# Scaling token tiles by 1/rms inside their transposing product, with a diagonal matrix in place of the identity

## The chip, the cores and the metric

The kernel runs on one core of one Trainium2 chip. The metric is device microseconds of one execution, the median over several runs. Engines are called as the profile calls them: PE is TensorE (PEld its weight loads), DVE is VectorE, ACT is ScalarE, POOL is GpSimd, SP is SyncE, which issues the transfers here.

## The reference

One layer of a hybrid backbone in float32: 1024 latent tokens `x` and 256 context tokens `ctx`, 1024 features each. Both are normed and modulated, multiplied by one input matrix, and feed a windowed attention and a bidirectional mLSTM; an output projection and a SwiGLU block follow. The change touches only the first step:

```python
def rms_norm(x, g):
    xf = x.astype(jnp.float32)
    y = xf * lax.rsqrt(jnp.mean(xf * xf, axis=-1, keepdims=True) + EPS)
    return (y * g.astype(jnp.float32)).astype(x.dtype)

def modulate(h, shift, scale):
    return h * (1.0 + scale) + shift

px = modulate(rms_norm(x, g_pre_mix[layer]), sh_m, sc_m) @ w_in[layer]
pc = modulate(rms_norm(ctx, g_pre_mix[layer]), csh_m, csc_m) @ w_in[layer]
```

A token has one factor 1/rms over all its features; gain, scale and shift are one number per feature.

## The kernel before, in words

Tokens are worked on in ten tiles of 128: tiles 0 to 7 are `x`, 8 and 9 are `ctx`. The projections need them transposed, features on partitions, and split into a high and a low part (`hh`, `hl`; `ch`, `cl` for the context) whose type, fp32r, takes one pass on TensorE; three products of such parts (lines 70 to 72) stand for one of full precision.

The first stage (line 224) multiplies the conditioning vectors by two sections of `w_ada`, streamed in eight tiles each; of the result come `scol` and `hcol`, one column of scale and of shift for each of 8 feature tiles (lines 235 to 249). With these each token tile i is prepared:

- `prep_a(i)`: load `xt` (line 183, one of four buffers, so tile i + 4 waits for tile i's last reader); ScalarE squares it and sums each row into `st` (line 185), writing its junk where `hraw` will be; square root and reciprocal give 1/rms, one number per partition (lines 176, 177); GpSimd multiplies `xt` by it in place (line 187).
- `prep_b(i)`: eight transposes of 128 x 128 against the identity `ident` (line 200), four to a tile `pt` in PSUM; VectorE multiplies each `pt` by `scol` into `hraw` (line 202); GpSimd, for tile 0 VectorE, adds `hcol` (line 203); `split` casts the high part on ScalarE (line 58) and subtracts for the low part on VectorE (line 59).
- `s1(i)`: 24 slab products of 272 columns (lines 70 to 72) give gates and some values (lines 277 to 282).

Then `gates()` works out the mLSTM gates in small steps, while TensorE runs a second slab of 384 columns for the ten tiles; `ml_weights` (lines 386 to 390) loads rows of the result, exponentiates and stores them, tile by tile. After that 13 projections of 128 columns follow in `tproj` (lines 441 to 444). The first two are convolved in `conv`: ScalarE copies the result out of PSUM to `cr` (lines 455, 458), VectorE makes three operations of it, first on 1024 latent columns, then on 256 context columns (lines 460 to 462). Beside them `ada_rest` takes the other sections of `w_ada` without TensorE: eight loads `wb` into two buffers and a product-and-add on VectorE for each (lines 491, 492; `wb_0` to `wb_7`).

The order on each engine is not the order of the code. A scheduler with its own model of the time writes it when the program is built; each engine then runs its list strictly in that order. So a change of one operation moves others.

Of the kernel before, what the change touches and what calls it, by code (L numbers as in the profile page):

```python
# [9 lines left out]
F32 = mybir.dt.float32  # L10
# [4 lines left out]
ADD, SUB, MUL, MAX, MIN = ALU.add, ALU.subtract, ALU.mult, ALU.max, ALU.min  # L15

P = 128
# [20 lines left out]
def body(tc, x, ctx, vecs, bcv, bada, gqm, gqf, wada, ws1, ws2, wt, wout, wfi, wfo,  # L38
         const, cosc, sinc, out):
    nc = tc.nc  # L40
    pe, act, dve, pool = nc.tensor, nc.scalar, nc.vector, nc.gpsimd
# [14 lines left out]
    def split(hi, lo, raw):  # L56

        act.copy(hi, raw)  # L58
        dve.tensor_tensor(lo, raw, hi.bitcast(F32), SUB)  # L59
# [18 lines left out]
    def hcast(t, n=4, w=P):  # L78

        return t.rearrange("p (h o) -> p h o", o=1).broadcast_to([t.shape[0], n, w])  # L80
# [13 lines left out]
    st = c.tile([P, 64], F32, name="st")  # L94
# [9 lines left out]
    ident = cst[:, CID:CID + P]  # L104
# [14 lines left out]
    def R(k, name, shape, dt=F32):  # L119
        t = rp[1].tile([P, 1152 if k < 4 else 1024], dt, name=name, tag=f"r{k}")  # L120
        n = int(np.prod(shape))
        v = t[:, 0:n]
        if len(shape) == 2:
            v = v.rearrange("p (a b) -> p a b", b=shape[1])
        elif len(shape) == 3:
            v = v.rearrange("p (a b c) -> p a b c", b=shape[1], c=shape[2])
        elif len(shape) == 4:
            v = v.rearrange("p (a b c d) -> p a b c d", b=shape[1], c=shape[2], d=shape[3])
        return v
# [28 lines left out]
    q1 = p1[1]  # L158
    w1h = [q1.tile([P, 4, 384], F32R, name=f"w1h{i}")[:, :, 0:272] for i in range(2)]
    w1l = [q1.tile([P, 4, 384], F32R, name=f"w1l{i}")[:, :, 0:272] for i in range(2)]  # L160

    q1.tile([P, 64], F32, name="padw")
    cs4 = q1.tile([P, KT, 4], F32R, name="cs4")
    cz4 = q1.tile([P, KT, 4], F32, name="cz4")
# [4 lines left out]
    def w2_tile(part, i, name):  # L169
        return q1.tile([P, 4 * 384], F32R, name=name, tag=f"w2{part}{i}")  # L170

    xts, hraw, xd = {}, {}, {}

    def rms_r(dst, ss):

        act.activation(dst, ss, AF.Sqrt, bias=epst, scale=1.0 / D)
        dve.reciprocal(dst, dst)

    def prep_a(i):

        j = i - NT
        xt = xts[i] = R(4 + i % 4, f"xt{i}", (D,))
        xd[i] = dma(xt, x[i * P:(i + 1) * P] if i < NT else ctx[j * P:(j + 1) * P])
        hraw[i] = R((12, 13, 8, 9, 10, 11)[i % 6], f"hraw{i}", (KT, P))
        act.activation(hraw[i].rearrange("p a b -> p (a b)"), xt, AF.Square, accum_out=st[:, i:i + 1])
        rms_r(st[:, 10 + i:11 + i], st[:, i:i + 1])
        pool.tensor_scalar(xt, xt, st[:, 10 + i:11 + i], 1.0, MUL, MUL)

    def prep_b(i):

        xt = xts.pop(i)
        q, j = (0, i) if i < NT else (1, i - NT)
        hs, ls = (hh, hl) if i < NT else (ch, cl)
        tok = slice(j * P, (j + 1) * P)
        rw = hraw.pop(i)
        for b in range(2):
            pt = pa.tile([P, 4, P], F32, name="pt", tag="tp", bufs=2)
            for k in range(4):
                kk = 4 * b + k
                pe.transpose(pt[:, k, :], xt[:, kk * P:(kk + 1) * P], ident)  # L200
            raw = rw[:, 4 * b:4 * b + 4]
            dve.tensor_tensor(raw, pt, hcast(scol[:, q, 4 * b:4 * b + 4]), MUL)
            (dve if i == 0 else pool).tensor_tensor(raw, raw, hcast(hcol[:, q, 4 * b:4 * b + 4]), ADD)
            split(hs[b][:, :, tok], ls[b][:, :, tok], raw)
# [6 lines left out]
    for sec in (1, 0):  # L211
        pr = [pa.tile([4, 512], F32, name=f"pr{sec}{i}", tag="mm", bufs=4) for i in range(2)]
        for kt in range(KT):
            w = R((8, 9, 10, 11, 12, 13)[(kt + 2 * (1 - sec)) % 6], f"wa{sec}_{kt}", (D,))
            wd = dma(w, wada[kt * P:(kt + 1) * P, sec * D:(sec + 1) * D])
            if kt % 2:
                wh, wl = (w2_tile(p, kt // 2 % 2, f"wa{p}{sec}_{kt}")[:, 0:D] for p in "hl")
                split(wh, wl, w)
                ops = ((cs4, wh), (cs4, wl))
            else:  # L220
                ops = ((cz4, w),)
            for n, (a, b) in enumerate(ops):
                for i in range(2):
                    pe.matmul(pr[i], a[:, kt, :], b[:, i * 512:(i + 1) * 512], start=kt == 0,
                              stop=kt == KT - 1 and n == len(ops) - 1)
            if (sec, kt) == (1, 0):
                with tc.issue_after(wd.ins):
                    dma(cst, const)
                    dma(bcr, bcast(bcv))
                dve.tensor_scalar(mF, up, -1.0, -NEG, ADD, MUL)  # L230
                dve.tensor_scalar(mB, lw, -1.0, -NEG, ADD, MUL)
            if (sec, kt) == (0, 4):
                prep_a(0)
# [52 lines left out]
    with tc.issue_after(wd.ins):  # L286
        for n in range(1, 4):
            prep_a(n)
    for n in range(2):
        prep_b(n)  # L290
    for i in range(NI):
        if i + 4 < NI:
            prep_a(i + 4)
        if i + 2 < NI:
            prep_b(i + 2)
        s1(i)
        if i in (5, 6):
            b = i - 5
            w2h.append(w2_tile("h", b, f"w2h_{b}").rearrange("p (k n) -> p k n", k=4))
            w2l.append(w2_tile("l", b, f"w2l_{b}").rearrange("p (k n) -> p k n", k=4))  # L300
            with tc.issue_after(xd[NI - 1].ins):
                slab_load(w2h[b], w2l[b], ws2[:, b], 384, 0)
# [286 lines left out]
    for j, name in enumerate(TILES):  # L589
# [5 lines left out]
        i = int(name[-1]) if name[-1].isdigit() else 0  # L595
# [49 lines left out]
        if 0 <= j - 3 < 9:  # L645
            s_ = j - 3
            if s_ >= 1 and s_ % 2 == 1:
                k = (s_ - 1) // 2
# [1128 lines left out]
```

## Time and profile before

| | |
|---|---|
| median of 3 runs | 1234.12 us (1230.72 to 1235.18) |
| the profiled execution | 1231.71 us |
| its span | 1229.9 us, 16238 instructions |
| PE busy | 1193.5 us (97%) |
| DVE, ACT, POOL busy | 799.9, 578.1, 205.8 us |
| first transposes of token tiles | 34.0 us |
| first and last slab product of 272 columns | 42.2 and 91 us |

Rows of a group give line, engine, operation, tiles (out<-in) and shapes, how often, then busy time and the mean length in ns, then the idle time of the engine ahead of them and what ended it. Rows of a timeline give start and length in us, then the same names; in brackets stands the idle time ahead and its releaser. Rows of one line or tile give the shortest, median and longest duration in ns. Rows of stretches give the busy time of each engine, the clock that was granted to TensorE, and the load of the transfers.

### The profile page before, as it was taken

The numbers are of one execution on the slowest core, as the hardware profiler recorded it, in microseconds if no ns is written. First come the engines' busy times: TensorE is split into PE (matmuls) and PEld (weight loads), VectorE is DVE, ScalarE is ACT, GpSimd is POOL, SyncE is SP. The second block draws the span as 40 slices with busy tenths as digits, with TensorE's granted clock in tenths as the row PEclk, the third lists the DMA queues.
The fourth block names the chain that finished last, engine by engine and source line by source line (L and its number), as shares of the span: only waits on it lengthen the run. The fifth ranks groups of instructions, "written<-read, shape, count | busy, mean of one in ns | idle before, by whom it ended". The sixth has DMA issues, their size and how long they took to land.

```text
span 1229.9 us, 16238 instructions
## 1 busy us (share of the span) xinstructions
PE 1193.5 (97%) x5859; PEld 968.9 (79%) x5859; DVE 799.9 (65%) x1385; ACT 578.1 (47%) x1105; POOL 205.8 (17%) x245
## 2 busy tenths in 40 slices
PE   7889999999999998999999999999999999999997
PEld 1779878877777776887778888888888888888886
DVE  3882177772877788446867677767777755554567
ACT  3754533211766786587643333334333334444443
POOL 0651410235544476000000000000000000000000
PEclk9899999999999999999999999999999999999999
DMA  8542854556533320522034465575645548665853
GB/s 313 168 132 70 280 188 144 181 145 191 153 90 87 112 78 10 188 86 86 18 104 136 180 218 198 204 246 195 230 141 177 176 162 279 205 205 188 299 188 129
DMA packets 91096, 202.30 MB, mean 164 GB/s; under 512 B 9092, under 2 KB 29956, under 8 KB 89608
## 3 DMA queue, kind: packets, MB, share of 16 engines
q1 hardware_dynamic: 91016, 201.27, 49.4%
q8 instruction: 46, 0.75, 0.2%
q14 instruction: 34, 0.28, 0.1%
HBM read 149.85 MB, written 50.73 MB: 163 GB/s over the span
## 4 chain that ended last, share of the span: by engine, by line
PE 78%; DMA 7%; DVE 7%; POOL 3%; ACT 3%; issue 2%; SPq 1%; DVEq 0%; POOLq 0%; ACTq 0%
PE xv L72 8%; PE xv L70 8%; PE xv L71 8%; PE pt L70 5%; PE pt L71 5%; PE pt L72 5%; PE pt L708 2%; PE pt L707 2%; PE pt L808 2%; DMA wb<-in_wada 2%; PE op L72 2%; PE fx L70 2%; PE fx L71 2%; PE fx L72 2%; PE op L71 2%
## 5 line engine op out<-in xcount | busy, mean ns | idle before, releaser
L59 DVE TENSOR_TENSOR fo<-fr,fo 128x1024 fp32r<-128x1024 f32 x77 | 92.7, 1222 | 70.9 <-ACT fo L58 67.7
L58 ACT CAST fo<-fr 128x1024 fp32r<-128x1024 f32 x77 | 79.5, 1050 | 74.0 <-PE pt L72 34.9
L441 PE MATMUL t<-hh,th 128*128 128x512 f32 x208 | 82.5, 397 | 1.8 <-ACT cr L458 1.8
L442 PE MATMUL t<-hl,th 128*128 128x512 f32 x208 | 82.1, 395 | 0.0
L1192 ACT CAST wS<-wr 128x512 fp32r<-128x512 f32 x88 | 54.1, 622 | 55.8 <-PE pt L72 37.5
L1194 DVE TENSOR_TENSOR wS<-wr,wS 128x512 fp32r<-128x512 f32 x88 | 60.3, 688 | 20.7 <-ACT wS L1192 20.7
L444 PE MATMUL t<-hh,tl 128*128 128x512 f32 x208 | 68.2, 393 | 0.0
L70 PE MATMUL xv<-tT,wS 128*128 128x512 f32 x168 | 66.0, 393 | 0.0
L72 PE MATMUL xv<-tT,wS 128*128 128x512 f32 x168 | 65.6, 391 | 0.0
L71 PE MATMUL xv<-tT,wS 128*128 128x512 f32 x168 | 65.5, 390 | 0.0
L492 DVE SCALAR_TENSOR_TENSOR acc<-wb,csil,acc 128x1024 f32<-128x1024 f32 x24 | 33.9, 1411 | 40.6 <-DMA wb<-in_wada 40.6
L441 PEld LDWEIGHTS t<-hh,th 128*128 128x128 f32 x208 | 39.1, 188 | 10.4 <-ACT cr L458 2.4
L944 DVE TENSOR_TENSOR wr<-wr 128x512 f32<-128x512 f32 x66 | 45.5, 689 | 1.4
L442 PEld LDWEIGHTS t<-hl,th 128*128 128x128 f32 x208 | 39.1, 188 | 8.1 <-issue 1.2
L1226 ACT ACTIVATE es<-es 128x512 f32<-128x512 f32 x22 | 13.9, 633 | 66.6 <-DVE es L947 66.6
L72 PE MATMUL op<-woh,ml 128*128 128x512 f32 x112 | 43.8, 391 | 0.8 <-DVE ml L59 0.8
L444 PEld LDWEIGHTS t<-hh,tl 128*128 128x128 f32 x208 | 38.3, 188 | 7.9 <-issue 1.0
L70 PE MATMUL op<-woh,mh 128*128 128x512 f32 x112 | 44.2, 395 | 0.0
L71 PE MATMUL op<-wol,mh 128*128 128x512 f32 x112 | 43.7, 390 | 0.0
L70 PE MATMUL pt<-fo 128*128 128x512 f32 x110 | 42.8, 389 | 0.0
L71 PE MATMUL pt<-fo 128*128 128x512 f32 x110 | 42.8, 389 | 0.0
L72 PE MATMUL pt<-fo 128*128 128x512 f32 x110 | 42.8, 389 | 0.0
(991 smaller groups left out, 3489.9 us busy)
## 6 DMA issues: line engine op xcount, KB each, us to landing
wr<-in_wfi SPq DMA_DIRECT2D x44, 512.0 KB, 4.8
wb<-in_wada SPq DMA_DIRECT2D x24, 512.0 KB, 4.3
s_d<-a SPq DMA_DIRECT2D x22, 512.0 KB, 6.6
bt<-in_wfo SPq DMA_DIRECT2D x44, 256.0 KB, 3.7
tb_d<-bt SPq DMA_DIRECT2D x11, 1024.0 KB, 4.1
fr<-s_d SPq DMA_DIRECT2D x44, 256.0 KB, 4.5
fr<-tb_d SPq DMA_DIRECT2D x44, 256.0 KB, 4.3
fr<-a_d SPq DMA_DIRECT2D x33, 256.0 KB, 4.2
```

The costliest lines, as they stand in the source:

```text
L58: act.copy(hi, raw)
L59: dve.tensor_tensor(lo, raw, hi.bitcast(F32), SUB)
L70: pe.matmul(ps, a[0], b[0], start=first, stop=False, **kw)
L71: pe.matmul(ps, a[0], b[1], start=False, stop=False, **kw)
L72: pe.matmul(ps, a[1], b[0], start=False, stop=last, **kw)
L441: pe.matmul(o, wh[:, kt], m[0], start=f, stop=False)
L442: pe.matmul(o, wh[:, kt], m[1], start=False, stop=False)
L444: pe.matmul(o, wl[:, kt], m[0], start=False, stop=l)
L492: dve.scalar_tensor_tensor(a, t, csil[:, kt, 0:1], a, MUL, ADD)
L944: dve.tensor_tensor(out, a, b, SUB)
L1192: act.copy(w[:, 0], raw)
L1194: dve.tensor_tensor(w[:, 1], raw, w[:, 0].bitcast(F32), SUB)
```

## The change

GpSimd no longer scales the token tile. It scales the identity by the same column of 1/rms, which gives a diagonal matrix `dg` of 128 x 128, and line 201 (200 before) multiplies the unscaled tile by it in place of transposing it: the product of the tile's transpose with the diagonal is the transposed, scaled tile. The transpose instruction becomes a plain matrix product in float32. `dg` has four buffers, which get their place beside the other tiles of this stage. One line is added at line 187, so later lines are one higher.

```diff
+    q1.tile([P, P], F32, name="dgx", tag="dg", bufs=4)
...
-        pool.tensor_scalar(xt, xt, st[:, 10 + i:11 + i], 1.0, MUL, MUL)
+        dg[i] = q1.tile([P, P], F32, name=f"dg{i}", tag="dg", bufs=4)
+        pool.tensor_scalar(dg[i], ident, st[:, 10 + i:11 + i], 1.0, MUL, MUL)
...
-        xt = xts.pop(i)
+        xt, dg_ = xts.pop(i), dg.pop(i)
...
-                pe.transpose(pt[:, k, :], xt[:, kk * P:(kk + 1) * P], ident)
+                pe.matmul(pt[:, k, :], xt[:, kk * P:(kk + 1) * P], dg_, start=True, stop=True)
```

The scheduler writes another order for the first 170 us; behind that the orders of all engines are the same. On TensorE 24 products of line 201 stand ahead of the first slab product, where 16 transposes did, and later ones stand eight together, where most stood four and four. On SyncE all loads of `ml_weights` come ahead of `cost`, `sint` and `wb_0`, where the last four loads stood among these or behind `wb_1`.

ScalarE at the first token tiles, before. The number behind `hraw`, `xt` and `hh` is the token tile, for `hh` the feature half; `L185` is the square, `L58` the cast of a high part.

```order
L185 ACTIVATE hraw4_372,st_67<-xt4_370 128x1024
L58 CAST w1h1_122<-wr272_22_309 128x2x272
L176 ACTIVATE st_67<-st_67,epst_61 128x1
L58 CAST hh0_101<-hraw0_250 128x4x128
L58 CAST hh1_102<-hraw0_250 128x4x128
L185 ACTIVATE hraw3_329,st_67<-xt3_327 128x1024
L58 CAST hh0_101<-hraw1_315 128x4x128
L176 ACTIVATE st_67<-st_67,epst_61 128x1
L185 ACTIVATE hraw5_427,st_67<-xt5_425 128x1024
```

And there in the changed program:

```order
L185 ACTIVATE hraw4_377,st_67<-xt4_375 128x1024
L176 ACTIVATE st_67<-st_67,epst_61 128x1
L185 ACTIVATE hraw5_433,st_67<-xt5_431 128x1024
L58 CAST hh0_101<-hraw1_317 128x4x128
L176 ACTIVATE st_67<-st_67,epst_61 128x1
L58 CAST hh0_101<-hraw0_251 128x4x128
L185 ACTIVATE hraw3_333,st_67<-xt3_331 128x1024
```

The square of tile 5 has moved ahead of every cast of a high part, and tile 1's first cast ahead of tile 0's.

VectorE at the first convolution, before. `ct` is what the convolution makes of `cr`, with 1024 columns and then 256; `acc` takes up `wb_0` to `wb_7`.

```order
L460 TENSOR_SCALAR ct<-cr,vec 128x1024
L461 SCALAR_TENSOR_TENSOR ct<-cr,vec,ct 128x1024
L492 SCALAR_TENSOR_TENSOR acc_1663<-wb_2_1671,csil,acc_1663 128x1024
L462 SCALAR_TENSOR_TENSOR ct<-cr,vec,ct 128x1024
L492 SCALAR_TENSOR_TENSOR acc_1663<-wb_3_1674,csil,acc_1663 128x1024
L460 TENSOR_SCALAR ct<-cr,vec 128x256
L461 SCALAR_TENSOR_TENSOR ct<-cr,vec,ct 128x256
L492 SCALAR_TENSOR_TENSOR acc_1663<-wb_4_1677,csil,acc_1663 128x1024
L462 SCALAR_TENSOR_TENSOR ct<-cr,vec,ct 128x256
```

And there in the changed program:

```order
L493 SCALAR_TENSOR_TENSOR acc_1674<-wb_2_1682,csil,acc_1674 128x1024
L461 TENSOR_SCALAR ct<-cr,vec 128x1024
L493 SCALAR_TENSOR_TENSOR acc_1674<-wb_3_1685,csil,acc_1674 128x1024
L462 SCALAR_TENSOR_TENSOR ct<-cr,vec,ct 128x1024
L493 SCALAR_TENSOR_TENSOR acc_1674<-wb_4_1688,csil,acc_1674 128x1024
L463 SCALAR_TENSOR_TENSOR ct<-cr,vec,ct 128x1024
L493 SCALAR_TENSOR_TENSOR acc_1674<-wb_5_1691,csil,acc_1674 128x1024
L461 TENSOR_SCALAR ct<-cr,vec 128x256
L493 SCALAR_TENSOR_TENSOR acc_1674<-wb_6_1694,csil,acc_1674 128x1024
L462 SCALAR_TENSOR_TENSOR ct<-cr,vec,ct 128x256
L463 SCALAR_TENSOR_TENSOR ct<-cr,vec,ct 128x256
```

The convolution's last operation, on 256 columns, stood behind the product with `wb_4` and stands behind that with `wb_6` now.

More of the change, by code (lines that the diff above doesn't have):

```diff
@@ L170, in w2_tile @@
         return q1.tile([P, 4 * 384], F32R, name=name, tag=f"w2{part}{i}")
-    xts, hraw, xd = {}, {}, {}
+    xts, hraw, xd, dg = {}, {}, {}, {}
     def rms_r(dst, ss):
```

## The prediction

> **What bounds the kernel now.** I read the page first, then the busy time by stretches, the timeline of TensorE through the stage that the change touches, and the waits of the engines that feed it.
>
> ```profile
> PE 1193.5 (97%) x5859; PEld 968.9 (79%) x5859; DVE 799.9 (65%) x1385; ACT 578.1 (47%) x1105; POOL 205.8 (17%) x245
> 34.00:45.00 11.00, 7.53 (x41) 6.14 (x41) 10.54 (x22) 8.83 (x19) 5.33 (x4) 0.70 0.60 208
> 45.00:84.00 39.00, 33.94 (x260) 32.04 (x260) 34.71 (x68) 23.51 (x52) 32.28 (x27) 1.00 0.41 125
> 113.00:164.00 51.00, 49.55 (x269) 44.71 (x267) 14.49 (x15) 28.00 (x81) 22.53 (x23) 1.00 0.78 261
> 164.00:300.00 136.00, 135.69 (x719) 108.95 (x721) 89.16 (x126) 32.36 (x47) 39.02 (x54) 1.00 0.56 165
> ```
>
> The first row is the page's, the others are stretches (length, then busy PE, PEld, DVE, ACT, POOL, clock). TensorE works 97% of the span, so what the change adds there is paid unless idle time takes it up. From 164 to 300 us it is busy 135.69 of 136: a delay before that is handed on whole. The token tiles are prepared from 34 to 84 us. There TensorE is busy 7.53 of 11 and 33.94 of 39 us, VectorE 34.71 and GpSimd 32.28: three engines near full, with little to win for any one.
>
> The timeline of TensorE shows where it waits (start, length; in brackets the idle time and who ended it):
>
> ```profile
> 37.80 0.41 PE L239 MATMUL pcol<-cst,r 4*128 4x4 f32 x4 [0.76 <-DVE r L236]
> 39.08 1.97 PE L200 MATMUL pt<-cst,xt 128*128 128x128 f32 x8 [0.88 <-POOL xt L187]
> 42.23 0.60 PE L70 MATMUL slab<-w1h,hh 128*128 128x272 f32 x1 [1.19 <-ACT hh L58]
> 45.21 0.28 PE L72 MATMUL slab<-w1h,hl 128*128 128x272 f32 x1
> 45.34 0.29 PE L70 MATMUL slab<-w1h,hh 128*128 128x272 f32 x1
> 68.85 0.39 PE L72 MATMUL slab<-w1h,hl 128*128 128x272 f32 x1 [0.56 <-DVE hl L59]
> 72.09 0.39 PE L72 MATMUL slab<-w1h,hl 128*128 128x272 f32 x1 [1.02 <-DVE hl L59]
> 75.15 0.39 PE L72 MATMUL slab<-w1h,hl 128*128 128x272 f32 x1 [0.85 <-DVE hl L59]
> 78.26 0.40 PE L72 MATMUL slab<-w1h,hl 128*128 128x272 f32 x1 [0.90 <-DVE hl L59]
> 83.81 0.39 PE L70 MATMUL slab<-w1h,ch 128*128 128x272 f32 x1 [1.50 <-ACT ch L58]
> 164.31 0.50 PE L441 MATMUL t<-hh,th 128*128 128x512 f32 x1 [1.76 <-ACT cr L458]
> ```
>
> Two kinds of loss can be seen: a slow start up to 45 us (waits, and a mean clock of 0.70), and five later waits for the split tiles, together 0.56 + 1.02 + 0.85 + 0.90 + 1.50 = 4.8 us. After those there is one more, 1.76 us at 164.
>
> **What the change removes.** Ten scalings of a whole token tile on GpSimd:
>
> ```profile
> L187 POOL TENSOR_SCALAR xt<-xt,st x10: 1117/1550/1566, 32.2 to 68.2; 128x1024 f32<-128x1024 f32 x10
> L637 POOL TENSOR_SCALAR bcr<-bcr 128x8 f32<-128x8 f32 x1 | 0.2, 203 | 6.1 <-DMA bcr<-in_bcv 6.1
> L59 DVE TENSOR_TENSOR hl<-hraw,hh x15: 672/957/1523, 44.1 to 76.8; 128x512 fp32r<-128x512 f32 x15
> ```
>
> The scaling lasts 1.12 to 1.57 us. The new one has an eighth of the elements; the trace has none of that size, so it lies between the same operation on 8 columns (0.20) and the shortest old one (1.12). I take 0.3, near the lower row, since 1.12 / 8 is 0.14. GpSimd gets back some 11 us. The third row shows a second gain: one and the same VectorE subtraction takes 0.67 to 1.52 us, and the long ones stand beside GpSimd's work. Both gains only shorten the path where TensorE waits for them, so they can return the 4.8 us, not 11. I take 4.3 as returned; nothing to 4.8 is the range.
>
> **What it adds on TensorE.** Eighty transposes become eighty plain fp32 products.
>
> ```profile
> L200 PE MATMUL pt<-cst,xt x80: 270/273/473, 34.0 to 80.2; 128*128 128x128 f32 x80
> 57.68 0.60 PE L200 MATMUL pt<-cst,xt 128*128 128x128 f32 x4
> L508 PE MATMUL ar<-one,acc x32: 170/250/251, 193.5 to 227.5; 128*128 128x1 f32 x32
> 193.45 1.84 PE L508 MATMUL ar<-one,acc 128*128 128x1 f32 x16
> 325.26 0.53 PEld L693 LDWEIGHTS s<-mq,mk 64*128 64x128 f32 x8 [0.24 <-issue]
> 321.63 0.49 PE L708 MATMUL pt<-V,wl 128*128 128x129 f32 x2
> 322.05 0.49 PE L707 MATMUL pt<-cs,qp 64*128 64x129 f32 x2
> ```
>
> A transpose is one pass (80 records for 80). At full clock four take 0.60, one lasts 0.27, so they follow each other at (0.60 - 0.27) / 3 = 0.11 us. A plain fp32 product is two passes: L508 is written 16 times and has 32 records. Its price, full weights and one moving column: (1.84 - 0.25) / 15 = 0.106 a pass, 0.21 a product. L693 moves 128 columns, four passes behind one another on each half of the rows; its weight loads (0.19 each) step by (0.53 - 0.19) / 3 = 0.11, so 0.22 a product. L708 and L707, which take turns on unequal numbers of rows, need 322.05 - 321.63 = 0.42 a product. The change has equal shapes in a row, as L508 and L693 have: I take 0.22, 0.11 more than now, 80 x 0.11 = 8.8 us; the ends are 8.0 (0.21) and 24.8 (0.42).
>
> [...]
>
> **The start.** The scheduler puts the first 24 products ahead of all slab products, and on ScalarE the square of tile 5 ahead of the first split. That square needs xt5's load, which needs xt1's buffer, which tile 1's products free.
>
> ```profile
> 34.96 1.06 ACT L185 ACTIVATE hraw<-xt 128x1024 f32<-128x1024 f32 x1 [0.44 <-DMA xt<-in_x]
> 36.49 0.29 ACT L176 ACTIVATE st<-st,epst 128x1 f32<-128x1 f32 x1
> 35.87 1.28 DVE L202 TENSOR_TENSOR hraw<-pt,scol 128x512 f32<-128x512 f32 x2
> xt<-in_x SPq DMA_DIRECT2D x16, 512.0 KB, 4.5
> 55.74 0.62 ACT L58 CAST hh<-hraw 128x512 fp32r<-128x512 f32 x1 [0.21 <-POOL hraw L203]
> ```
>
> Tile 1's reciprocal stands behind two L202 on VectorE (35.87 + 1.28 = 37.2), the diagonal takes 0.3, the products start near 37.7 and take 8 x 0.22 = 1.8 at full or 3.6 us at half clock: done at 39.5 to 41.3, say 40.5. Then the load, 4.5 (45.0), the square, 1.06, a cast, a square root and tile 0's cast, 0.6 + 0.3 + 0.6: the first slab product at 47.5, between 46.5 and 48.3. Before, the sixth began at 45.21 with the same 24 transposes behind it; five steps of 0.13 earlier is 44.6. So 2.9 us later, and 0.6 for a clock that may still be half after so long a wait: +3.5, between 1.9 and 5. ScalarE runs in order: behind the waiting square stand all casts of the first tiles, for them VectorE's splits, and for these the slabs. The other new waits cost nothing that I can see: a diagonal's buffer comes round after four tiles, whose products are long done, and no transfer is added or taken away.
>
> **The slabs.** The other 56 products stand among them: 56 x 0.11 = 6.2. With the start 3.5 and the waits returned 4.3, TensorE ends this phase 3.5 + 6.2 - 4.3 = 5.4 us later.
>
> **The wait at 164.** It would take up 1.76 of that, if its releaser came as early as now. But VectorE's order moves there too: the context part of the first convolution stands behind the product with wb_6 now, before behind that with wb_4.
>
> ```profile
> 161.65 1.28 DVE L492 SCALAR_TENSOR_TENSOR acc<-wb,csil,acc 128x1024 f32<-128x1024 f32 x1 [0.66 <-DMA wb<-in_wada]
> 162.85 0.48 DVE L462 SCALAR_TENSOR_TENSOR ct<-cr,vec,ct 128x256 f32<-128x256 f32 x1
> 163.69 0.57 ACT L458 COPY cr<-t 128x512 f32<-128x512 f32 x1
> 166.96 1.28 DVE L492 SCALAR_TENSOR_TENSOR acc<-wb,csil,acc 128x1024 f32<-128x1024 f32 x1 [1.46 <-DMA wb<-in_wada]
> ```
>
> wb_4's product is the row at 161.65, wb_6's that at 166.96. With loads as now the latter ends at 168.2, two operations of 0.48 and the copy of 0.57 follow, and TensorE goes on near 169.8, 5.5 us later than at 164.31. On SyncE the loads of wb_0 and wb_1 now stand behind all loads of the ml weights, with later stores of these weights still behind them, which may move them two or three us either way: 3.6 (TensorE alone, 5.4 - 1.8) to 8. I take **+5.5 us**. From there the rows of 164 to 300 leave nothing to take it up.
>
> **The sum.** The profiled execution took 1231.71 us (span 1229.9 and 1.8 around it): 1231.7 + 5.5 = 1237.2. It lay 2.4 under the median of the three runs, 1234.12; for a median I say **1239.6**. This is +0.45%; about 0.5%, 6.2 us, is what a measurement of this kernel can tell from no change.
>
> **Rivals.**
> (a) The clock does not fall. The 24 early products run at full clock and so do the first slabs: tile 1 is done at 39.5, the start costs 1.5 in place of 3.5, and the loads behind follow: +1.5 to +3.5, 1235.6 to 1237.6. For it: before, TensorE stood idle three times from 36 to 39 and the clock of the stretch was 0.70, and there is more work now. Against: a wait of some 5 us remains ahead of the first slab. Chance 0.2. [...]
> (b) Slower, on the other side of "no change": the diagonal products do not overlap their weight loads and cost 0.42, as L708 and L707 do. Then 16 us come on top, 1239.6 + 16 = 1256. It decides as soon as eight of them take over 3 us at full clock (1.8 in my forecast). For it: it is the only fp32 row with 128 rows and 128 moving columns. Against: its neighbours change the shape each time. Chance 0.12.
> (c) The convolution waits longer: wb_0 starts later, and the pairs come 2.7 us apart (161.65, 164.21, 166.96). One step more is +8 to +9: 1242.5. Chance 0.13.
> (d) GpSimd is what paces 45 to 84, busy 32.28 of 39. Seven of its scalings, 7 x 1.1 = 7.7 us, would go: 1226. Against: TensorE alone needs 33.94 + 6.2 = 40.1 us for that work, more than the 39 it has now, so the stretch can't shrink. Chance 0.05.
>
> **How the numbers follow.** The forecast has 0.5, (a) 0.2, (b) 0.12, (c) 0.13, (d) 0.05. Of the forecast's band, +3.6 to +8, I count 0.3 within 0.5% and 0.2 above. Faster: 0.04, from (d). Within: 0.3 + 0.2 + 0.01 = 0.51. Slower: 0.2 + 0.12 + 0.13 = 0.45. The range, 1233 to 1248, leaves out (b) and (d), 0.17.
>
> **What would show it.** Line 201 has 160 records, x8 in about 2 us at full clock; GpSimd's ten diagonals near 0.3 us; the first slab product at 46.5 to 48.3 us, released by ScalarE behind the square of tile 5; no waits on hl between 68 and 79; the first L441 behind the convolution near 170. If line 201's eight take over 3 us, (b) holds; if the first slab starts before 45.5 and L441 goes on before 167, (a); if TensorE still waits for hl, the 4.3 were wrong.

## The result, and the profile after

The changed kernel takes 1240.02 us (median of 5 runs, 1237.89 to 1242.74); before, measured beside it, takes 1232.64 us (5 runs, 1230.72 to 1235.18). The ratio is 1.0064, with a 95% interval of 1.0045 to 1.0084: slower by 0.64%, or 7.9 us, and by 7.4 us if the medians are subtracted. The forecast was +5.5 us and 1239.6. The level was hit more closely than the difference, because before came out 1.5 us lower than its first three runs had shown: that part is luck. By the prediction's own bound of 0.5% this is "slower", to which it had given 0.45, against 0.51 for a change within the bound.

The profiled execution of after is its slowest (1242.74), 2.7 us above the median. Its mean granted clock is 0.94, where the other four have 0.99. Most of that is only the reading: its full level reads 0.95 in place of 1.00, and yet the products of the second slab start 0.173 us apart in both profiles. A stretch at 0.50 from 319.05 to 325.87 us, which before does not have, is real, and goes with some 2.7 us behind the first product ar.

The share and the stretches of after, the rows that answer to those of before:

```profile
PE 1206.1 (97%) x5939; PEld 982.6 (79%) x5939; DVE 795.5 (64%) x1385; ACT 577.2 (47%) x1105; POOL 191.6 (15%) x245
```

```profile
34.00:45.00 11.00, 8.40 (x62) 6.45 (x60) 8.37 (x20) 6.46 (x14) 1.78 (x4) 0.95 0.69 212
45.00:84.00 39.00, 36.13 (x279) 35.94 (x280) 29.36 (x60) 22.92 (x50) 20.41 (x23) 0.87 0.35 114
113.00:164.00 51.00, 51.00 (x281) 47.07 (x281) 9.28 (x16) 27.32 (x79) 21.30 (x19) 0.95 0.72 246
164.00:300.00 136.00, 132.54 (x699) 106.33 (x698) 92.76 (x129) 33.37 (x48) 35.01 (x47) 0.94 0.53 158
```

GpSimd has lost 11.9 of its 32.3 us between 45 and 84 us, VectorE 5.3. The wait that stood in the stretch up to 164 is gone from it and stands in the next one, where TensorE now lacks 3.5 us (before 0.3). Of each clock in these rows, 0.05 is missing by the lower reading alone.

Three groups that the change makes or alters, and below them VectorE's subtraction in before (the columns behind the bar are busy us and mean ns):

```profile
L201 PE MATMUL pt<-dg,xt 128*128 128x128 f32 x160 | 20.0, 279 | 1.0 <-POOL dg L188 0.9 <-issue 0.2
L59 DVE TENSOR_TENSOR hl<-hraw,hh 128x512 fp32r<-128x512 f32 x16 | 12.1, 769 | 0.5 <-ACT hh L58 0.5
L188 POOL TENSOR_SCALAR dg<-cst,st 128x128 f32<-128x128 f32 x10 | 5.5, 557 | 36.1 <-DVE st L177 36.1
```

```profile
L59 DVE TENSOR_TENSOR hl<-hraw,hh 128x512 fp32r<-128x512 f32 x16 | 17.3, 1084 | 4.1 <-ACT hh L58 4.1
```

160 records for 80 products: two passes each, as forecast (the 240 slab products of 272 columns, in fp32r, left 240). VectorE's subtraction for hl is at 769 ns on average, from 1084. The diagonals take 557 ns on average, not 300 (their median is 374, the longest takes 1421).

The timeline of TensorE at the start and at the convolution (start, length, idle time before and who ended it):

```profile
34.70 2.06 PE L201 MATMUL pt<-dg,xt 128*128 128x128 f32 x16
38.08 2.06 PE L201 MATMUL pt<-dg,xt 128*128 128x128 f32 x16 [0.39 <-POOL dg L188]
40.07 0.66 PE L240 MATMUL pcol<-cst,r 4*128 4x4 f32 x8
41.20 2.06 PE L201 MATMUL pt<-dg,xt 128*128 128x128 f32 x16 [0.47 <-POOL dg L188]
47.71 0.59 PE L70 MATMUL slab<-w1h,hh 128*128 128x272 f32 x1 [4.45 <-ACT hh L58]
...
169.41 0.79 PE L442 MATMUL t<-hh,th 128*128 128x512 f32 x1 [3.46 <-ACT cr L456]
```

Sixteen passes take 2.06 us. Behind the first, whose successor starts 0.21 us later, they start 0.112 us apart, so a product costs 0.224 and a second pass 0.112 us. Their 16 weight loads take 1.87 us (34.69 to 36.56) beside them. From the first slab product to 169 no wait of over 0.2 us is left. The five waits of before among the slabs are gone. The wait ahead of the first slab is 4.45 us, where it was 1.19, and that at the convolution 3.46, where it was 1.76.

Why the first slab waits is seen on VectorE and ScalarE:

```profile
41.82 0.18 DVE L242 COPY col<-pcol 128x32 f32<-128x32 f32 x1
43.40 0.16 DVE L177 RECIPROCAL st<-st 128x1 f32<-128x1 f32 x1 [1.41 <-ACT st L176]
43.48 0.23 DVE L245 TENSOR_TENSOR hcol<-col 128x8 f32<-128x8 f32 x2
44.96 2.12 DVE L204 TENSOR_TENSOR hraw<-hraw,hcol 128x512 f32<-128x512 f32 x2
```

```profile
41.90 1.06 ACT L185 ACTIVATE hraw<-xt 128x1024 f32<-128x1024 f32 x1 [1.56 <-DMA xt<-in_x]
43.08 0.29 ACT L176 ACTIVATE st<-st,epst 128x1 f32<-128x1 f32 x1
45.30 1.06 ACT L185 ACTIVATE hraw<-xt 128x1024 f32<-128x1024 f32 x1 [1.93 <-DMA xt<-in_x]
47.06 0.60 ACT L58 CAST hh<-hraw 128x512 fp32r<-128x512 f32 x1
```

Three things stand in one another's way. pcol, from which the shift hcol comes, is transposed behind tile 1's products (40.07; before at 37.80, ahead of them). hcol then stands on VectorE behind the reciprocal of tile 3, which waits for that tile's load and square (43.40). Last comes the square of tile 5 at 45.30, ahead of tile 0's cast at 47.06. I had named only the last.

Around the convolution, on VectorE, in SyncE's queue and on ScalarE:

```profile
160.29 1.28 DVE L493 SCALAR_TENSOR_TENSOR acc<-wb,csil,acc 128x1024 f32<-128x1024 f32 x1 [2.69 <-DMA wb<-in_wada]
161.49 0.75 DVE L461 TENSOR_SCALAR ct<-cr,vec 128x1024 f32<-128x1024 f32 x1
165.52 1.29 DVE L493 SCALAR_TENSOR_TENSOR acc<-wb,csil,acc 128x1024 f32<-128x1024 f32 x1 [0.89 <-DMA wb<-in_wada]
166.72 1.28 DVE L463 SCALAR_TENSOR_TENSOR ct<-cr,vec,ct 128x1024 f32<-128x1024 f32 x1
```

```profile
148.18 5.57 SPq L391 DMA_DIRECT2D w_dr<-w  x2
155.17 1.65 SPq L492 DMA_DIRECT2D wb<-in_wada  x2
```

```profile
168.04 1.06 ACT L464 ACTIVATE mk<-ct 128x1024 f32<-128x1024 f32 x1 [11.48 <-DVE ct L463]
169.00 0.35 ACT L456 COPY cr<-t 128x256 f32<-128x256 f32 x1
173.38 0.57 ACT L459 COPY cr<-t 128x512 f32<-128x512 f32 x1
```

The first operation of the convolution (L461) now stands behind the product with wb_2, and wb_2's load stands on SyncE behind two stores of ml weights that wait for their data until 153.7. Each further step of the convolution alternates with such a product, and some of these wait for their load (0.89 us at 165.52). L463, the last step on the latent columns, stands behind the product with wb_4 and frees the buffer cr. ScalarE then takes the convolution's Silu (L464) and behind it copies the context columns to cr (L456). For that copy TensorE waits.

### The profile page after: what moved, and what is told of

Same layout as the page of the kernel before. It is cut to its first block, busy times and chain, and to the rows that moved or that the text cites. A ratio compares the mean times of both kernels' runs of the same rounds, so it can differ in the third digit from the quotient of the medians.

```text
span 1241.0 us, 16410 instructions
## 1 busy us (share of the span) xinstructions
PE 1206.1 (97%) x5939; PEld 982.6 (79%) x5939; DVE 795.5 (64%) x1385; ACT 577.2 (47%) x1105; POOL 191.6 (15%) x245
## 4 chain that ended last, share of the span: by engine, by line
PE 80%; DMA 7%; DVE 5%; ACT 3%; POOL 2%; issue 2%; SPq 1%; DVEq 0%; POOLq 0%; ACTq 0%
PE xv L72 8%; PE xv L70 8%; PE xv L71 8%; PE pt L70 5%; PE pt L71 5%; PE pt L72 5%; PE pt L709 2%; PE pt L708 2%; PE pt L809 2%; DMA wb<-in_wada 2%; PE fx L70 2%; PE t L442 2%; PE t L443 2%; PE t L445 2%; PE fx L72 2%; PE fx L71 2%
## 5 line engine op out<-in xcount | busy, mean ns | idle before, releaser
L58 ACT CAST fo<-fr 128x1024 fp32r<-128x1024 f32 x77 | 79.6, 1051 | 74.0 <-PE pt L72 36.5
L779 PE MATMUL s<-k,qh 128*128 128x256 f32 (+1 forms) x128 | 42.2, 339 | 1.8 <-ACT so L624 1.0
L70 PE MATMUL pt<-fo 128*128 128x512 f32 x110 | 42.8, 389 | 0.0
L71 PE MATMUL pt<-fo 128*128 128x512 f32 x110 | 42.8, 389 | 0.0
```

The source lines that it names most:

```text
L70: pe.matmul(ps, a[0], b[0], start=first, stop=False, **kw)
L71: pe.matmul(ps, a[0], b[1], start=False, stop=False, **kw)
L779: pe.matmul(o, qh[:, h, :], k2[g][:, kc], start=True, stop=False)
```

## Where the time lies

A table by stage, worked out from the starts in each profiled execution: from the first transposing product to the first slab product, from there to the first product t (L441 in before, one line on in after), and from there to the first product ar (L508). Behind that, up to the last product, every kernel takes 1030.0 to 1031.7 us (after 1033.05, see above), so nearly all that these kernels differ in lies in the three columns. One execution each: their sums agree with the ratios only within about 3 us, and the ratios decide.

| kernel | to the slab | slabs | t to ar | sum | ratio to before (95%) |
|---|---|---|---|---|---|
| before | 8.27 | 90.49 | 60.73 | 159.5 | 1 |
| after | 13.01 | 90.26 | 63.76 | 167.0 | 1.0064 (1.0045 to 1.0084) |
| e1 products only | 12.03 | 89.13 | 62.52 | 163.7 | 1.0017 (1.0003 to 1.0031) |
| e7 one pass | 7.29 | 87.83 | 60.33 | 155.5 | 0.9957 (0.9941 to 0.9973) |
| e2 square held | 11.56 | 91.92 | 65.26 | 168.7 | 1.0055 (1.0039 to 1.0071) |
| e5 start held | 11.23 | 87.69 | 63.45 | 162.4 | 1.0036 (1.0021 to 1.0051) |
| e3 stores on ScalarE | 13.21 | 90.47 | 62.90 | 166.6 | 1.0044 (1.0028 to 1.0061) |
| e6 convolution held | 12.11 | 91.25 | 62.37 | 165.7 | 1.0028 (1.0016 to 1.0041) |
| e11 both held | 11.03 | 88.40 | 58.91 | 158.3 | 0.9999 (0.9988 to 1.0010) |
| e9 tiles 3 to 9 | 7.87 | 90.86 | 66.97 | 165.7 | 1.0042 (1.0030 to 1.0054) |
| e10 tiles 0 to 2 | 11.00 | 89.28 | 59.92 | 160.2 | 1.0005 (0.9995 to 1.0015) |
| e4 scaling on ScalarE | 9.71 | 87.74 | 60.73 | 158.2 | 0.9972 (0.9959 to 0.9985) |
| e8 e4, orders held | 9.84 | 88.28 | 64.92 | 163.0 | 1.0004 (0.9992 to 1.0015) |
| e12 ScalarE from tile 3 | 7.80 | 85.70 | 61.50 | 155.0 | 0.9959 (0.9946 to 0.9971) |

The border between the first two columns is not the same in all rows. In after, e1, e2, e3, e5, e6, e10 and e11 tile 2's eight products stand ahead of the first slab product; in before, e7, e9 and e12 they stand behind it (in e4 and e8 half of them), and count as slabs. In before they take 1.56 us there, at half clock (they start 0.21 us apart, and 0.11 at full clock).

## The experiments

### What a second pass costs: e1 and e7

e1 is before with the products alone:

```
-                pe.transpose(pt[:, k, :], xt[:, kk * P:(kk + 1) * P], ident)
+                pe.matmul(pt[:, k, :], xt[:, kk * P:(kk + 1) * P], ident, start=True, stop=True)
```

> Before with one edit: the 80 transposes become plain fp32 products with the identity; GpSimd still scales the whole token tiles, and nothing is relieved. Theory A (GpSimd's relief gave the waits on hl back): the second passes cost 80 x 0.112 = 9 us, the waits of 4.8 us stay, so +8 to +9 us against before. Theory B (the second passes fill the waits by themselves, since a wait ends when VectorE's split is done and TensorE then arrives later): the waits shrink from 4.8 to under 1.5 us with the relief absent too, so +4 to +5.5 us. In both, line 201's eight take 1.8 to 2.0 us at the full clock.

Measured: 1234.46 us, +0.17%, some 2 us. In the stretch of the slabs, by busy time (TensorE's first), and in the group of GpSimd's scalings:

```profile
45.00:84.00 39.00, 39.00 (x312) 38.94 (x312) 31.65 (x63) 21.92 (x49) 25.97 (x23) 0.96 0.36 117
```

```profile
L187 POOL TENSOR_SCALAR xt<-xt,st 128x1024 f32<-128x1024 f32 x10 | 15.0, 1509 | 29.9 <-DVE st L177 28.1 <-DVE G L279 1.7
```

TensorE is busy 39.00 of 39 us, although GpSimd still scales whole tiles (15.0 us). Theory B has the mechanism, and the cost is lower than its +4 to +5.5: the second passes themselves fill the waits for hl, with no relief of GpSimd. The late start of e1 (12.03 us) is not what fills them: e10, below, starts nearly as late (11.00) with whole scalings and one-pass transposes among the slabs, and still waits 4.6 us there.

e7 is after with one pass: the transposes wait for the same tile from GpSimd as in after. It leaves out the scaling by 1/rms:

```
-        pool.tensor_scalar(dg[i], ident, st[:, 10 + i:11 + i], 1.0, MUL, MUL)
+        pool.tensor_scalar(dg[i], ident, st[:, 10 + i:11 + i], 0.0, MUL, ALU.is_gt)
-                pe.matmul(pt[:, k, :], xt[:, kk * P:(kk + 1) * P], dg_, start=True, stop=True)
+                pe.transpose(pt[:, k, :], xt[:, kk * P:(kk + 1) * P], dg_)
```

> After with the products made one-pass transposes: GpSimd's operation compares the scaled identity with zero, so that it costs and waits as in after but yields the identity; left out is the scaling of the tokens by 1/rms. Theory A (each second pass counts in full): 80 x 0.112 = 9 us less, so after -8 to -9, that is before -1 to +1. Theory B (the second passes mostly stand where TensorE would wait for VectorE's splits anyway, as the run with the products alone, +2.5 us in place of +8 to +9, hints): waits on hl of 2 us or more in all are back between 45 and 84 us, and the time is after -3 to -6.

Measured: 1226.56 us, 0.43% faster than before and 13 us faster than after. Neither theory had this size. With shorter products the scheduler writes another order again: pcol ahead of tile 1, a slab ahead of tile 2 (7.29 us to the slab), and short waits at the convolution. By stage, e7 lies 5.7, 2.4 and 3.4 us below after. In the last of these stages no product of line 201 stands, so 3.4 us at least are not passes but order; how the rest divides between passes and order is not shown. Of the waits for hl, these two are the largest:

```profile
71.64 0.39 PE L72 MATMUL slab<-w1h,hl 128*128 128x272 f32 x1 [0.86 <-DVE hl L59]
75.69 0.39 PE L72 MATMUL slab<-w1h,hl 128*128 128x272 f32 x1 [1.10 <-DVE hl L59]
```

All idle time among its slabs sums to 2.6 us, against 5.1 before. So GpSimd's relief without second passes goes with half of the waits returned, where the second passes without relief (e1) left none. The relief is smaller here than in after: GpSimd, which does the comparing, is busy 27.81 of the 39 us from 45 to 84, and 20.41 in after.

### The start: e2 and e5

e2 is after with the square of tile 5 held:

```
         if i + 4 < NI:
-            prep_a(i + 4)
+            with ExitStack() as hold:
+                if i == 1:
+                    hold.enter_context(tc.issue_after(casts[0].ins))
+                prep_a(i + 4)
```

(casts[0] is tile 0's second cast to hh; issue_after queues what the block holds behind it on the same engine.)

> After with one edit: on ScalarE the square and the square root of tile 5 are queued behind the second cast of tile 0; SyncE's order stays. Theory A (the start's 4.45 us of wait comes from the square of tile 5 that waits for its load): the first slab product starts at 44 to 45.5 us in place of 47.7, and the time falls by 2 to 3 us against after. Rival C (the stretch from 45 to 84 is paced by VectorE and GpSimd, and TensorE only waits later): the first slab starts earlier but waits on hl come back, and the time stays within 1 us of after.

Measured: 1239.97 us, a ratio of 1.0055, whose interval overlaps that of after. The first slab starts at 44.26 us, inside theory A's range, but the first product also came 2.0 us earlier in this execution; behind that product the slab starts 1.5 us earlier. And TensorE waits for hl instead:

```profile
44.26 0.60 PE L71 MATMUL slab<-w1h,hh 128*128 128x272 f32 x1 [3.02 <-ACT hh L58]
46.50 0.59 PE L73 MATMUL slab<-w1h,hl 128*128 128x272 f32 x1 [0.97 <-DVE hl L59]
```

Rival C is right here: the square, my one reason for the late start, is not what the start is worth.

e5 holds pcol and hcol as well:

```
     with tc.issue_after(wd.ins):
         for n in range(1, 4):
-            prep_a(n)
+            with ExitStack() as hold:
+                if n == 3:
+                    hold.enter_context(tc.issue_after(hcol_last.ins))
+                prep_a(n)
     for n in range(2):
-        prep_b(n)
+        with ExitStack() as hold:
+            if n == 1:
+                hold.enter_context(tc.issue_after(pcol_last.ins))
+            prep_b(n)
```

> After with three orders held at the start and nothing else: tile 1's products stand behind the transposes of pcol on TensorE, tile 3's reciprocal behind the shift hcol on VectorE, tile 5's square behind tile 0's casts on ScalarE. Theory A2 (the first slab is late because hcol, which tile 0's split needs, stands behind the late pcol and behind tile 3's reciprocal, which waits for its load): from the first product to the first slab 9 to 10.5 us in place of 13.0, and the time falls by 2.5 to 4 us against after. Rival C (VectorE and GpSimd then pace the first slabs, as the 0.97 us wait on hl in the run with the square alone held hints): the slabs start earlier but wait on hl, and the time stays within 1 us of after.

Measured: 1234.91 us, a ratio of 1.0036, 3.4 us better than after, in the range of theory A2; the intervals of the two ratios just overlap (1.0051 against 1.0045). TensorE's waits, the convolution's among them:

```profile
36.05 0.74 PE L242 MATMUL pcol<-cst,r 4*128 4x4 f32 x8 [0.44 <-ACT r L238]
39.99 2.02 PE L203 MATMUL pt<-dg,xt 128*128 128x128 f32 x16 [1.22 <-POOL dg L190]
43.86 0.39 PE L71 MATMUL slab<-w1h,hh 128*128 128x272 f32 x1 [1.85 <-ACT hh L58]
162.46 0.50 PE L453 MATMUL t<-hh,th 128*128 128x512 f32 x1 [2.93 <-ACT cr L467]
```

The start itself is 1.8 us shorter, less than the 2.5 that I had written at the least. The slabs are 2.6 us shorter, which is what the clock accounts for: in e5 the first slab products start 0.13 us apart, and the clock from 36 to 46 us is 1.00, where after has 5.1 us at 0.50 among its slabs (47.71 to 52.81), half of which is 2.6. The convolution still waits 2.93 us.

### The convolution: e3 and e6

e3 is after with the eight stores of the ml weights issued by ScalarE:

```
-        dma(w_dr[n], wt_.rearrange("p d h t -> p (d h t)"))
+        act.dma_start(w_dr[n], wt_.rearrange("p d h t -> p (d h t)"))
```

> After with one edit: the eight stores of the ml weights are issued by ScalarE, which computes these weights, in place of SyncE; VectorE's and GpSimd's orders are word for word those of after. Theory A (the wait of 3.46 us at 169 is that of the loads wb_2 and wb_3, which stand on SyncE behind two stores that wait for the weights): wb_2 is issued 3 us or more earlier than at 155.2, the wait before line 442 falls below 1.5 us, and the time falls by 2 to 3.5 us against after. Rival D (the wb loads are paced by their two buffers and by the 2.6 us that a load takes, wherever they are issued): the wait stays above 2.5 us and the time within 1 us of after.

Measured: 1238.91 us, a ratio of 1.0044, better than after by 0.2 points, with intervals that overlap.

```profile
168.05 0.66 PE L442 MATMUL t<-hh,th 128*128 128x512 f32 x1 [2.39 <-ACT cr L456]
```

The wait falls from 3.46 to 2.39, neither below 1.5 nor unchanged. The stores ahead of wb_2 explain a third of it. The rest I put down to the loads' own pace, and to VectorE's order, which puts the products with them ahead of the convolution; e6 tests the second.

e6 turns that order round:

```
+            conv_first.setdefault(seg, cl_)
...
+                with ExitStack() as hold:
+                    if sec == 4 and kt >= 2:
+                        hold.enter_context(tc.issue_after(conv_first[1].ins))
+                    dve.scalar_tensor_tensor(a, t, csil[:, kt, 0:1], a, MUL, ADD)
-                dve.scalar_tensor_tensor(a, t, csil[:, kt, 0:1], a, MUL, ADD)
```

(cl_ is the convolution's last VectorE operation, conv_first[1] that of the first convolution's context part.)

> After with one order held: on VectorE the products with wb_2 to wb_7 of that section stand behind the whole first convolution; the first 400 rows of the other engines' orders are those of after. Theory E (TensorE's wait of 3.46 us at 169 is the convolution's wait for the loads wb_2 to wb_5, and the half clock of 3.4 us behind it is its echo): the wait falls below 1 us, the clock stays up, and the time falls by 3 to 5.5 us against after. Rival F (the copies and the second convolution, now behind later products, take its place): another wait of 2 us or more stands between 160 and 185 us, and the time stays within 1.5 us of after.

Measured: 1235.39 us, a ratio of 1.0028, 4.4 us better than after. The wait at 169 is gone, another is there:

```profile
181.38 0.50 PE L442 MATMUL t<-hh,th 128*128 128x512 f32 x1 [1.81 <-ACT cr L456]
```

Theory E has the size, F a part of the picture: the second convolution now stands between the late loads and costs 1.81 us. The profiled execution is the slowest of the twelve (1238.61) and shows only 1.4 us of the gain between t and ar; the size rests on the median. Up to the convolution the orders are those of after, so the edit acts at this place alone.

### Both orders at once: e11, and e8

e11 is after with the edits of e5 and of e6.

> After with both orders held that were held one at a time: pcol, hcol and the square at the start, and the first convolution ahead of wb_2 to wb_7. If the two gains (3.4 and 4.4 us) lie in different places they add up: before -1 to +1.5 us (ratio 0.999 to 1.001). Rival F (the loads behind a convolution that now comes earlier only move the wait to the second convolution, as held orders did with ScalarE scaling): before +2.5 to +4.5 us.

Measured: 1231.86 us, a ratio of 0.9999 (0.9988 to 1.0010). The two gains add up, the mean granted clock of the profiled execution is 1.0 (before 0.996), and no wait is left at the convolution. So with the order held at two places nothing of the 0.64% is left that can be measured. The longer products themselves do not have to cost it. That they cost nothing in themselves is not shown: e11 also lacks the wait of 1.76 us that before has at the convolution (58.91 us from t to ar, against 60.73), and before was not run with that order held.

e8 makes the same edits, but for the square, on the kernel of e4 (below), which scales on ScalarE.

> The kernel with the token tiles scaled on ScalarE and one-pass transposes, with the orders of the two runs above held: pcol ahead of tile 1, hcol ahead of tile 3's reciprocal, and the first convolution ahead of wb_2 to wb_7. That kernel without the held orders was 0.28% faster than before. Theories A2 and E: 1.5 to 3 us less than it, so before -4 to -6 us (ratio near 0.996). Rivals C and F: the waits only move, and the ratio stays at 0.9965 to 0.998.

Measured: 1232.4 us, a ratio of 1.0004: slower than without the edits (0.9972). The waits move, as rivals C and F say, but the loss is outside their range of 0.9965 to 0.998 too. TensorE waits for 5.1 us in all between t and ar, against 1.7 in e4. Holding an order helps where that order is what waits, and costs where it is not.

### Early and late tiles: e9 and e10

Both choose by tile between the two ways, e9 with `i >= 3`, e10 with `i < 3`. The scaling is shown here; the instruction of line 201 follows the same choice:

```
+        if i >= 3:
+            dg[i] = q1.tile([P, P], F32, name=f"dg{i}", tag="dg", bufs=4)
+            pool.tensor_scalar(dg[i], ident, st[:, 10 + i:11 + i], 1.0, MUL, MUL)
+        else:
+            pool.tensor_scalar(xt, xt, st[:, 10 + i:11 + i], 1.0, MUL, MUL)
```

> The change for tiles 3 to 9 alone; tiles 0 to 2 are scaled and transposed as before, and VectorE's, ScalarE's and TensorE's orders at the start are those of before. The products with wb stand ahead of the first convolution as in after. Theory G (the loss lies in the start and in the convolution's wait; the second passes among the slabs only fill waits): the first slab starts 8 to 8.7 us after the first transpose, as before; 56 x 0.112 = 6.3 us of second passes stand against some 5 us of waits that go; the convolution's wait is 2.5 us or more: before +1 to +4 us. Rival H (the second passes count in full): before +6 us or more.

Measured: 1237.66 us, +0.42% or 5 us, between theory G's upper end and rival H. The start and the slabs are as G has them (7.87 us, and 90.86 against 90.49: 6.3 us of passes against 4.8 of waits that went). The convolution is far worse than I had thought:

```profile
166.03 0.80 PE L448 MATMUL t<-hh,th 128*128 128x512 f32 x1 [4.41 <-ACT cr L462]
```

A wait of 4.41 us, and 6.8 us of half clock that begin in its last part: with a start like that of before, the late tiles alone lose 6 us between t and ar.

> The change for tiles 0 to 2 alone; tiles 3 to 9 are scaled on GpSimd and transposed as before. The order at the start is that of after: 24 products ahead of the first slab, pcol behind tile 1's products, hcol behind tile 3's reciprocal, the square of tile 5 ahead of tile 0's casts. Theory G (the start carries about half of the loss): the first slab starts 12.5 us or more after the first product, the later waits on hl shrink by 1 to 3 us since VectorE and GpSimd get ahead of a late TensorE: before +2 to +4 us. Rival H (the late start is made good in the slabs, where GpSimd and VectorE set the pace): before -1 to +1 us.

Measured: 1232.17 us, a ratio of 1.0005: no change. Rival H holds:

```profile
43.53 0.39 PE L70 MATMUL slab<-w1h,hh 128*128 128x272 f32 x1 [2.36 <-ACT hh L58]
45.60 0.60 PE L72 MATMUL slab<-w1h,hl 128*128 128x272 f32 x1 [1.55 <-DVE hl L59]
77.36 0.39 PE L72 MATMUL slab<-w1h,hl 128*128 128x272 f32 x1 [1.28 <-DVE hl L59]
```

The slab starts 2.7 us later, and the slabs (89.28) and the convolution (59.92) give 2.0 of it back. Part of this is only the border of the columns: tile 2's products now stand ahead of the first slab. That VectorE and GpSimd work on meanwhile and so make a late start good is not what the waits show: among the slabs they fall only from 5.1 to 4.6 us.

### A better place for the scaling: e4 and e12

e4 is before with the scaling of all ten tiles on ScalarE (the last line of this edit in place of the first); e12 is the same from tile 3 on:

```
-        pool.tensor_scalar(xt, xt, st[:, 10 + i:11 + i], 1.0, MUL, MUL)
+        if i < 3:
+            pool.tensor_scalar(xt, xt, st[:, 10 + i:11 + i], 1.0, MUL, MUL)
+        else:
+            act.activation(xt, xt, AF.Copy, scale=st[:, 10 + i:11 + i])
```

> Before with one edit: the ten scalings of a token tile (128x1024) run on ScalarE, not on GpSimd; the transposes stay one pass. Theory A (the 4.8 us of waits on hl come from GpSimd's work beside VectorE): ten more operations of about 1.06 us on ScalarE, which is busy 23.5 of 39 us there, cost nothing, the waits go, and the time falls by 3 to 5 us against before. Rival C (ScalarE's order becomes the chain: a scaling stands ahead of the casts of the tile before): TensorE waits for casts in place of splits, and the time is between -1 and +4 us of before.

Measured: 1229.47 us, a ratio of 0.9972, 3.4 us faster than before, as theory A has it; but the waits among the slabs are not gone, they sum to 2.7 us.

> Before with the scaling of tiles 3 to 9 on ScalarE and that of tiles 0 to 2 still on GpSimd, transposes of one pass. At the start the orders are those of before. Theory A (GpSimd's work among the slabs makes the waits on hl; ScalarE has room there): the start takes 8 to 8.7 us as before in place of the 9.7 with ScalarE alone, the waits on hl fall to 2.7 us or less: before -4 to -6 us. Rival C (ScalarE's scalings stand ahead of casts that TensorE waits for): before -3 us or less of a gain, no better than all ten on ScalarE (-3.4).

Measured: 1227.38 us, a ratio of 0.9959 (0.9946 to 0.9971): 5 us faster than before and 1.0% faster than after, with transposes of one pass.

```profile
L190 ACT ACTIVATE xt<-xt,st 128x1024 f32<-128x1024 f32 x7 | 8.1, 1152 | 0.4 <-DVE st L177 0.4
```

Theory A holds. Seven scalings, 8.1 us on ScalarE, cost TensorE nothing among the slabs, where it waits 1.2 us in all; the wait at the convolution grows from 1.76 to 2.48 us. This version beats both kernels.

## Why the prediction was right, and where it was not

The time came out within the range and on the side that was forecast, and most terms had their size. But the closeness of the level is luck, two reasons were wrong, and the delay at the convolution was too small.

**Two passes of 0.11 us.** Right: 160 records, eight products in about 2 us, and twice the price of a transpose (0.224 us against 0.11); rival (b) is out.

**The diagonals and hl.** The diagonals take 0.56 on average where I took 0.3; TensorE waits 0.9 us for them in all, at the start. hl fell from 1084 ns on average to 769, as meant.

**The waits returned, 4.3.** The size is right (none is left), the reason only in part. e1 shows the second passes filling the waits with GpSimd's work unchanged; in e7, with relief and one pass, half of the waits are gone. The two causes were claimed for the same 4.8 us, and one was enough.

**The start, +3.5.** The first slab at 47.71 lies within 46.5 to 48.3, and compared like with like (44.6 before, the sixth product moved up) it is 3.1 us later, or 2.4 if both are counted from the first transposing product, which came at 34.70 in after and at 33.96 in before. The chain was told wrongly: e2 takes the square out of the way and gains nothing that can be told from noise; pcol and hcol had to be held as well (e5).

**TensorE at the end of the slabs, +5.4.** It is +5.25: t begins at 137.97, against 132.72. Counted from the first transposing product it is +4.5.

**The wait at 164: here the prediction failed.** It said that TensorE "goes on near 169.8, 5.5 us later than at 164.31", and took 5.5 as the delay. It does go on at 169.41, but the agreement is chance. The copy that the forecast meant stands behind the convolution's context part and the product with wb_6 (L459). It starts only at 173.38, and no wait of TensorE ends with it. TensorE waits for another copy, that of the context columns (L456, 169.00). In before this copy was done ahead of the product that stands eight places ahead of the one at 164.31 and needs its place in PSUM:

```profile
159.66 0.35 ACT L455 COPY cr<-t 128x256 f32<-128x256 f32 x1
160.55 0.39 PE L441 MATMUL t<-hh,th 128*128 128x512 f32 x1
```

And the time at which a wait ends is the delay only if the same instruction waits. The wait stands further ahead in TensorE's program: 152 products t stood ahead of it before, 144 now. Eight products, 0.23 us each and 1.8 in all, that used to run ahead of the wait now come behind it. With the half clock, which lasts until 172.3 and so takes half of 2.9 us, or 1.4, that makes 5.1 + 1.8 + 1.4 = 8.3 us; the first ar comes 8.3 us later (201.73 against 193.45), or 7.5 counted from the first transposing product. Read the other way: the wait grew from 1.76 to 3.46 instead of being used up. Rival (c) had the place and the price (+8 to +9) at 0.13. The runs that hold the order there (e6, e11) show that it is this place.

**Rival (a)** was half right: the clock did not fall at 38.33, as it had before, but at 45.98, within the wait of 4.45 us that ends at 47.71. **Rival (d)** is out.

What stays open: how the start's 3.4 us divide between pcol, hcol, the square and the clock; why a late start costs that much in after and nothing in e10; what before would take with the convolution's order held; why e9 waits longest of all at the convolution; and why the held order costs in e8.

## What to carry to other kernels

Cost a longer instruction at the place where it stands: here 9 us of passes cost 2 us alone, for they filled waits that were already there, and the relief that was to pay for them was counted on the same waits. Then look at what the new lengths do to the order of everything around, wait by wait, and count for each wait which instruction stands behind it and how much work stands ahead of it, not only when it ends. A change that measures as a loss may be two misplaced instructions; hold their order before dropping it, and try the idle engine (here ScalarE, which before is busy 23.51 of the 39 us from 45 to 84) for the work as well.

## What the runs showed of the hardware that was not expected

**Half clock in before and after.** From 16 us on, apart from the last us of the work (from 1226.17 in before, from 1237.23 in after), the granted clock was 0.50 in before from 38.33 to 45.16 us, and in after from 45.98 to 52.81, 168.86 to 172.27 and 319.05 to 325.87 us. Each of these stretches lasted 3.41 or 6.83 us.

**The clock at a wait.** Behind TensorE's waits of 2.39 (e3), 2.93 (e5), 3.46 (after) and 4.41 us (e9) at the convolutions, products t of 512 columns started 0.43 us apart for a while, in place of 0.23; the mean clock from 164 to 174 us was 0.86 in e5, 0.80 in after (its full level reads 0.95) and 0.66 in e9. With a wait of 1.76 us (before) and two of 1.64 and 1.67 us (e1) it was 1.00 from 113 to 174 us, and behind 2.48 us (e12) the products started 0.23 us apart. So the length of the wait alone does not part these runs, 2.39 us against 2.48; what else decides is not shown.

**Transposes and the clock.** In before, e7, e9 and e12, which transpose the first tiles in one pass, the mean clock from 36 to 46 us was 0.66 (in e4, from 34 to 45, 0.69). With products in their place it was 0.99 in e1 and 1.00 in e5 and e6, and from 34 to 44 us 0.99 in e2 and 1.00 in e11 (in e3, from 34 to 45, 1.00); in after it held from 15.26 to 45.98. The 3.41 us ahead of the fall in before and in e7, and 3.41 us around 38 us in e5, by busy time (TensorE's first) and granted clock:

```profile
34.91:38.33 3.41, 1.88 (x16) 1.15 (x14) 2.98 (x7) 3.08 (x7) 0.42 (x1) 1.00 0.58 180
```

```profile
34.49:37.90 3.41, 1.91 (x16) 1.49 (x16) 2.95 (x11) 2.50 (x6) 1.86 (x2) 1.00 0.91 313
```

```profile
36.98:40.40 3.41, 2.19 (x19) 2.03 (x19) 2.89 (x10) 2.01 (x4) 1.07 (x2) 1.00 0.84 294
```

Ahead of the two falls TensorE was less busy, 1.88 and 1.91 us against 2.19 in e5. Whether this or the transposes themselves made the difference is not shown.

**Where a single profile begins.** In after the mean clock was 0.76 from 9 to 14 us and 0.89 from 14 to 24 (of 0.95); in e2, with the same program up to there, it was 1.00 in both. The first transposing product came at 34.70 us in after and at 32.70 in e2. So single profiles are compared from that product on.
